# A head's bonus sum from a rounded high and low part, in two passes instead of one fp32 matmul

## The chip, the cores and the metric

The kernel runs on one core of a Trainium2 chip. The metric is the time of one execution on the device in microseconds (us), the median of the runs shown. The engines are TensorE (PE in the profile, with its weight loads listed apart as PEld), VectorE (DVE), ScalarE (ACT), GpSimd (POOL) and SyncE (SP), which issues every DMA of this kernel from one queue in order. An engine executes its own instructions in the order in which they stand.

## The reference, cut to what matters

One layer of a hybrid trunk is computed for 1024 prompt tokens and 128 sample tokens (8 requests of 16). Branch A is an RWKV-7 time mixing with 16 heads of 64 channels. Of it, this case is about one line, the bonus:

```python
y, S = wkv7_scan(wkv0.astype(f32), r_h, w_h, kh_h, a_h, v_h, kt_h)
...
yn = yn * gn_w.astype(f32) + gn_b.astype(f32)
bonus = jnp.sum(r_h * kt_h * r_bonus.astype(f32), axis=-1, keepdims=True) * v_h
o_a = (yn + bonus.reshape(B_, T, WIDTH_A)).astype(x.dtype) * jax.nn.silu(z_a)
```

For each token and head the products r * kt * r_bonus are summed over the head's 64 channels, and the sum multiplies the value vector v. Besides this there are the combined input projection (81 blocks of 128 columns), the delta-rule scan, a short-convolution branch, three output projections, a gate and norms.

## The kernel before, in words

Activations lie with channels on the 128 partitions and tokens along the free axis. Branch A is worked in 24 steps: 8 pairs of heads (j), and for each pair three token blocks, 512 prompt tokens, the 128 sample tokens and the other 512 prompt tokens (`BLOCKS`). A step goes through coroutines: `prep` (projections k, r, v, z, the decay, then `keys`), `scores`, `values`, `inverse` (a block inverse in levels), `chain` (the recurrence, chunk by chunk of 64 tokens) and `tail`. Beside them run `conv` (the convolution branch, 8 times four projections) and, when that is through, `gates_b` (six projections of the merge gates). The dense matmuls of `prep`, `conv` and `gates_b` are the filling between the dependent matmuls of the chain.

The order of PE in this first stage is written out by `go()`: a planner that holds a clock `pe[0]`. `spent` adds a price for each matmul to it (by columns; fp32 at a quarter of the speed of everything else), each coroutine yields how long its next piece must wait, and `go()` takes the first stream that is ready, or else filling. So a change of a price in `spent` moves what is taken later. The other engines, and PE after the first stage, are ordered by the framework's scheduler.

The bonus goes as follows. `keys` writes `rkt` = r * r_bonus * kt on DVE (L494), a tile of one buffer. `values` later sums it over each head's channels with one fp32 matmul against `onesb`, a 128x128 matrix of two blocks of ones (L553; in the profile all matmuls but transposes have line L92, and this one is `psb<-rkt,cpk`), and DVE multiplies v by the result (L555).

Weights come in through `load_w` (L142): a staging tile `wst` of the ring with two buffers, one DMA of 512 KB, a cast to a high fp16 part on ACT (L148) and the rest as a low part on DVE (L149). The two small decay matrices of a pair come through `load_lora` (L341): four DMAs into `lw`, a tile of its own with one buffer, and the same split (L352, L353).

The second stage (from L946 on) has the remaining merge gates (`gate`, tiles `dgb` and `dga`), the projections `dense_r` of branch B (`ob`), branch A (`oa`) and the output (`oc`). Its operands are split by `split_r` into a high part in the rounded fp32 type (F32R) and a low part that is the difference (L955, L957), and its matmuls run on these. Its tiles lie in the memory that the first stage gave back, so the loads of `ob` start when the last tail of the first stage is through.

Of the kernel before, what the change touches and what calls it, by code (L numbers as in the profile page):

```python
# [9 lines left out]
F32 = mybir.dt.float32  # L10
F16 = mybir.dt.float16
F32R = mybir.dt.float32r
I32 = mybir.dt.int32
AF = mybir.ActivationFunctionType
ALU = mybir.AluOpType
# [4 lines left out]
KT = 8  # L20
# [3 lines left out]
RN = 512  # L24
# [42 lines left out]
def build(nc, tc, I, O):  # L67
    with ExitStack() as top:
        _build(nc, tc, I, O, top)


def _build(nc, tc, I, O, top):
    V, A, G, PE, SP = nc.vector, nc.scalar, nc.gpsimd, nc.tensor, nc.sync
# [5 lines left out]
    def spent(lhsT, rhs, f32):  # L79
        rows, m, n = lhsT.shape[0], cols(lhsT), cols(rhs)  # L80
        mode = (64 if rows <= 64 else 128, 64 if m <= 64 else 128)
        t = 2 * max(n / 1.2, m / 1.2) if f32 else max(n / 2.4 + 2, 28)
        if mode != (128, 128):
            t /= 2
        if mode != pe[1] and pe[1] is not None:
            t += 100
        pe[1] = mode
        pe[0] += t / 1000

    def mm(out, lhsT, rhs, start, stop):  # L90
        spent(lhsT, rhs, lhsT.dtype == F32)
        PE.matmul(out, lhsT, rhs, start=start, stop=stop)  # L92

    def tr(out, in_, ident_):
        pe[0] += 0.14
        PE.transpose(out, in_, ident_)
# [16 lines left out]
    def P(n, i):  # L113
        o, w = PN[n]
        return par[:, o + i:o + i + 1]
# [36 lines left out]
    wcur = [None, 6]  # L152
# [36 lines left out]
    rk = ExitStack()  # L189
# [11 lines left out]
    onesb, seq4, sm_p, sm_s, i64h, scan_p, scan_s = (C[n] for n in ("onesb", "seq4", "sm_p", "sm_s", "i64", "scan", "scan_s"))  # L201
# [6 lines left out]
    def cload():  # L208
        SP.dma_start(shs, I["shift"])
        SP.dma_start(packs[0], I["c_pack"])  # L210
        SP.dma_start(packs[1], I["c_packh"])
        SP.dma_start(cvs, I["conv"])

    wk = rk.enter_context(tc.tile_pool(name="wkv", bufs=2))
    cvp = rk.enter_context(tc.tile_pool(name="cvp", bufs=1))
    wcur[0] = rk.enter_context(tc.tile_pool(name="wpool", bufs=2))
    st_ = rk.enter_context(tc.tile_pool(name="stg", bufs=1))

    def tt(pool, tag, nm, bufs, n=RBUF):
        return pool.tile([128, n], F32, tag=tag, name=nm, bufs=bufs)  # L220
# [108 lines left out]
    def pair(j):  # L329
        if j not in pairs:  # L330
            pairs[j] = s = St()
            s.w, s.lora = {}, False
        return pairs[j]
# [7 lines left out]
    def load_lora(j):  # L341
        s = pair(j)
        if s.lora:
            return
        s.lora = True
        lw = st_.tile([128, 2, 128], F32, tag="lw", name=f"lw{j}", bufs=1)
        for hv in range(2):
            for q in range(2):
                SP.dma_start(lw[hv * 64:hv * 64 + 64, q, :], I["w_lora"][j, q * 64:q * 64 + 64, :])
        s.lwh = st_.tile([128, 2, 128], F16, tag="lwh", name=f"lwh{j}", bufs=2)  # L350
        s.lwl = st_.tile([128, 2, 128], F16, tag="lwl", name=f"lwl{j}", bufs=2)
        A.activation(s.lwh, lw, AF.Copy, scale=WS)  # L352
        V.scalar_tensor_tensor(out=s.lwl, in0=lw, scalar=WS, in1=s.lwh, op0=ALU.mult, op1=ALU.subtract)  # L353
# [8 lines left out]
    def hold(us):  # L362
        bank[bank.index(min(bank))] = pe[0] + us

    def prep(f):

        j, g = f.j, f.g
        f.s = s = pair(j)
        load_lora(j)
        if g == 0:  # L370
            s.sst = wk.tile([128, 8, 64], F32, tag="sst", name=f"sst{j}", bufs=1)
# [85 lines left out]
        if ahead:  # L457
            load_lora(j + 1)
# [8 lines left out]
    def keys(f, kh, kt, b2, r, pb, pi):  # L467
        j = f.j
        blk = o, n = f.blk
        smp, nch, npr, nm = f.smp, f.nch, f.npr, f.nm  # L470
        yield lambda: S_open.at == 3 and (f.i < 1 or steps[f.i - 1].kb_done)
        ar = wk.tile([128, nch, 2, 64], F32, tag="ar", name="ar" + nm, bufs=3)
        kb = wk.tile([128, npr, 4, 64], F32, tag="kb", name="kb" + nm, bufs=1)
        ar4 = ar.rearrange("p (c e) x t -> p c (e x) t", e=2)
        if smp:
            for dst, src, t0 in ((1, kh, 0), (0, r, 1)):
                for c in range(2):
                    x = dst if c == 0 else 1 - dst
                    V.tensor_tensor(out=ar[:, c, x, :].rearrange("p (s t) -> p s t", t=16),
                                    in0=src[:, c * 64:c * 64 + 64].rearrange("p (s t) -> p s t", t=16),  # L480
                                    in1=pb[:, 4 * c:4 * c + 4, t0:t0 + 16], op=ALU.mult)
        else:
            p4 = pb.rearrange("p (c e) t -> p c e t", e=2)
            s4 = lambda x: x.rearrange("p (c e t) -> p c e t", e=2, t=64)
            V.tensor_tensor(out=ar4[:, :, 1:3, :], in0=s4(kh), in1=p4[:, :, :, 0:64], op=ALU.mult)
            V.tensor_tensor(out=ar4[:, :, 0:4:3, :], in0=s4(r), in1=p4[:, :, :, 1:65], op=ALU.mult)
        pr2 = lambda x: x.rearrange("p (c e t) -> p c e t", e=2, t=64)
        pr1 = lambda x: x.rearrange("p (c t) -> p c t", t=128)
        V.tensor_tensor(out=kb[:, :, 0:4:3, :], in0=pr2(kt), in1=pr2(pi), op=ALU.mult)
        V.scalar_tensor_tensor(out=kb[:, :, 1:3, :].rearrange("p c e t -> p c (e t)"), in0=pr1(b2), scalar=0.5,  # L490
                               in1=pr1(pi), op0=ALU.mult, op1=ALU.mult)

        f.rkt = tt(wk, "rkt", "rkt" + nm, 1, RN)[:, :n]
        V.scalar_tensor_tensor(out=f.rkt, in0=r, scalar=P("rb", j), in1=kt, op0=ALU.mult, op1=ALU.mult)  # L494
        f.ar, f.kb = ar, kb

    def scores(f):
# [28 lines left out]
    def values(f):  # L526

        smp, nch, npr, nm = f.smp, f.nch, f.npr, f.nm
        kb, v, scx = f.kb, f.v, f.scx

        kbt = f.kbt = wk.tile([128, nch, 128], F32, tag="kbt", name="kbt" + nm, bufs=2)
        for c0 in range(0, nch, 4):
            yield 0.0, 1
            pk = psp.tile([128, 512], F32, tag="p", name=f"pk{nm}_{c0}")
            cn = min(4, nch - c0)
            for c in range(c0, c0 + cn):
                tr(pk[:, (c - c0) * 128:(c - c0 + 1) * 128],
                   kb[:, c // 2, 2 * (c % 2):2 * (c % 2) + 2, :].rearrange("p a b -> p (a b)"), ident)
            hold(1.2)
            A.activation(kbt[:, c0:c0 + cn, :].rearrange("p c f -> p (c f)"), pk[:, :cn * 128], AF.Copy)  # L540

        f.kb_done = True
        vu = f.vu = wk.tile([128, nch, 128], F32, tag="vu", name="vu" + nm, bufs=2)
        vu4 = f.vu4 = vu.rearrange("p (c e) f -> p c e f", e=2)
        yield 0.0
        pv = psa.tile([128, 512], F32, tag="a", name="pv" + nm)
        for i in range(npr):
            tr(pv[:, i * 128:(i + 1) * 128], v[:, i * 128:(i + 1) * 128], ident)
        pv3 = pv[:, :npr * 128].rearrange("p (c f) -> p c f", f=128)
        A.activation(vu4[0:64, :, 0, :], pv3[0:64], AF.Copy)  # L550
        A.activation(vu4[64:128, :, 1, :], pv3[64:128], AF.Copy)
        psb = psa.tile([128, 512], F32, tag="a", name="psb" + nm)
        mm(psb[:, :npr * 128], onesb, f.rkt, start=True, stop=True)  # L553
        f.bv = v
        V.tensor_tensor(out=v, in0=v, in1=psb[:, :npr * 128], op=ALU.mult)  # L555
        yield 1.6, 1
        x0p = psp.tile([128, 8, 64], F32, tag="p", name="x0" + nm)[:, :2 * npr, :]
        for p in range(npr):
            for h, H in enumerate(HS):
                for e in range(2):  # L560
                    mm(x0p[HS[1 - e], h * npr + p, :], scx[HS[e], h, p, e, :], vu[HS[e], 2 * p + e, H],
                       start=True, stop=True)
        hold(1.5)
        x04 = x0p.rearrange("p (h c) v -> p c h v", h=2)
        for e in range(2):
            A.activation(vu4[HS[1 - e], :, e, :].rearrange("p c (h v) -> p c h v", h=2), x04[HS[1 - e]], AF.Copy)
        f.x_done = True
# [277 lines left out]
    for j in range(8):  # L845
        for g in range(3):
            f = St()
# [10 lines left out]
    load_q(0, "k")  # L858
    wl = load_w(I["w_in"][T_L], "l")
    cload()  # L860
    load_lora(0)
    cws[0] = load_w(I["w_in"][T_C], "C0")
    load_q(0, "r")
# [85 lines left out]
    op = top.enter_context(tc.tile_pool(name="op", bufs=1))  # L949
# [51 lines left out]
    for j in range(KT):  # L1001
# [3 lines left out]
        for blk in BL3:  # L1005
            o, n = blk
            ps = dense_r(w, obs, blk, f"ob{j}_{o}")
            V.scalar_tensor_tensor(out=ms[j][:, o:o + n], in0=ms[j][:, o:o + n], scalar=1.0, in1=ps,
                                   op0=ALU.add, op1=ALU.mult)
# [14 lines left out]
    for j in range(KT):  # L1024
        w = load_wr(I["w_oa"][j], f"a{j}")
        g = gts[j]
        for blk in BL3:
            o, n = blk
# [233 lines left out]
```

## Time and profile before

| | |
|---|---|
| median of 3 runs | 1888.74 us (1888.63 to 1889.81) |
| the profiled execution | 1887.54 us, of it 1885.7 us span |
| PE busy | 1795.6 us, 95% of the span |
| DVE, ACT, POOL busy | 1250.5, 815.2, 210.8 us |
| the fp32 matmuls `psb` | 24 (16 of 512 columns, 8 of 128), each listed as two passes |

The page's first part gives the busy time of each engine. Its second part cuts the span in 40 slices and gives tenths of each, with the granted clock of TensorE below. The chain of waits (part 4) is followed back from the last instruction. In a timeline a row has its start, its length, engine, line, operation, what is written from what, how many instructions are merged in the row, and in brackets the idle time before it with what ended it. Matmuls overlap: a row's length is longer than its distance to the next row, and it is the distance that counts as the engine's time.

### The profile page before, as it was taken

The numbers are of one execution on the slowest core, as the hardware profiler recorded it, in microseconds if no ns is written. First come the engines' busy times: TensorE is split into PE (matmuls) and PEld (weight loads), VectorE is DVE, ScalarE is ACT, GpSimd is POOL, SyncE is SP. The second block draws the span as 40 slices with busy tenths as digits, with TensorE's granted clock in tenths as the row PEclk, the third lists the DMA queues.
The fourth block names the chain that finished last, engine by engine and source line by source line (L and its number), as shares of the span: only waits on it lengthen the run. The fifth ranks groups of instructions, "written<-read, shape, count | busy, mean of one in ns | idle before, by whom it ended". The sixth has DMA issues, their size and how long they took to land.

```text
span 1885.7 us, 37719 instructions
## 1 busy us (share of the span) xinstructions
PE 1795.6 (95%) x15326; PEld 1242.4 (66%) x15326; DVE 1250.5 (66%) x3181; ACT 815.2 (43%) x1871; POOL 210.8 (11%) x333
## 2 busy tenths in 40 slices
PE   5999999999999999999999999999999999999997
PEld 2555665565666666566566556565499777999865
DVE  5577887788688788788788878861422411545566
ACT  6454463554555446446446446442311311333332
POOL 1001121111112111111101101100000011200000
PEclk9999999999999999999999999999999999999998
DMA  6011102011111101101100200221512410242012
GB/s 223 12 35 49 53 17 76 22 33 54 36 33 48 52 31 42 60 31 36 63 31 24 76 29 16 64 86 64 170 58 65 133 45 23 85 157 91 13 32 79
DMA packets 45198, 110.65 MB, mean 59 GB/s; under 512 B 6368, under 2 KB 21344, under 8 KB 45024
## 3 DMA queue, kind: packets, MB, share of 16 engines
q1 hardware_dynamic: 45024, 108.24, 17.9%
q8 instruction: 120, 1.97, 0.4%
q14 instruction: 54, 0.44, 0.1%
HBM read 87.94 MB, written 20.28 MB: 57 GB/s over the span
## 4 chain that ended last, share of the span: by engine, by line
PE 66%; DVE 20%; ACT 7%; DMA 3%; issue 2%; POOL 1%; SPq 0%; DVEq 0%; ACTq 0%
PE ob L92 5%; PE oc L92 5%; PE oa L92 5%; PE dr L92 4%; PE pg L92 4%; PE dz L92 4%; PE dga L92 4%; PE dgb L92 4%; PE dk L92 3%; PE dB L92 3%; PE dzb L92 3%; PE dv L92 3%; PE u L92 2%; PE dC L92 2%; PE dx L92 2%
## 5 line engine op out<-in xcount | busy, mean ns | idle before, releaser
L92 PEld LDWEIGHTS <-whip 128*128 128x128 f16 x1536 | 132.7, 99 | 72.1 <-issue 6.5
L687 POOL TENSOR_SCALAR Spt<-sbd,pt 128x128 f32<-128x128 f32 x128 | 91.3, 713 | 612.0 <-DVE sbd L706 611.0
L706 DVE SCALAR_TENSOR_TENSOR sbd<-u,pt,Spt 64x64 f32<-64x64 f32 x256 | 72.1, 282 | 68.7 <-PE u L92 65.7
L92 PEld LDWEIGHTS <-wlop 128*128 128x128 f16 x768 | 75.5, 98 | 61.8 <-issue 2.2
L92 PE MATMUL dgb<-hx,whigb 128*128 128x512 f16 (+1 forms) x480 | 110.4, 326 | 3.9 <-ACT ms L993 3.5
L627 ACT ACTIVATE bdgt<-ig 64x512 f16<-64x512 f32 (+1 forms) x208 | 106.5, 512 | 2.7
L92 PE MATMUL dB<-hx,whiB 128*128 128x512 f16 (+1 forms) x384 | 90.5, 331 | 4.4 <-ACT sho L233 4.4
L92 PE MATMUL dx<-hx,whiX 128*128 128x512 f16 (+1 forms) x384 | 90.1, 328 | 2.8 <-ACT sho L240 2.8
L92 PE MATMUL dC<-hx,whiC 128*128 128x512 f16 (+1 forms) x384 | 89.9, 328 | 2.1 <-ACT sho L233 2.1
L92 PE MATMUL dzb<-hx,whiZ 128*128 128x512 f16 (+1 forms) x384 | 88.1, 326 | 3.4 <-ACT sho L233 1.7
L92 PE MATMUL dv<-hx,whip 128*128 128x512 f16 (+1 forms) x384 | 90.1, 329 | 0.9 <-DVE zb L829 0.9
L694 ACT ACTIVATE yst<-c 64x128 f32<-64x128 f32 x144 | 38.9, 270 | 119.4 <-DVE xs L693 117.6
L92 PE MATMUL dz<-hx,whip 128*128 128x512 f16 (+1 forms) x384 | 90.5, 329 | 0.0
L92 PE MATMUL dr<-hx,whip 128*128 128x512 f16 (+1 forms) x384 | 90.0, 329 | 0.0
L92 PE MATMUL dk<-hx,whip 128*128 128x512 f16 (+1 forms) x384 | 88.1, 326 | 0.0
L92 PEld LDWEIGHTS <-pg 128*128 128x128 f16 x768 | 65.7, 99 | 27.7 <-issue 3.2
L620 ACT ACTIVATE gt<-ig 128x512 f16<-128x512 f32 (+1 forms) x104 | 54.2, 521 | 67.1 <-PE ig L92 66.6
L628 DVE CAST_PREDICATED tt<-cph,i 128x512 f16<-128x512 uint16 (+1 forms) x104 | 61.8, 594 | 29.9 <-PE i L92 26.0
L700 ACT ACTIVATE vu<-u 64x64 f32<-64x64 f32 x288 | 62.7, 218 | 39.8 <-PE u L92 36.2
L92 PE MATMUL dgb<-hx,wlogb 128*128 128x512 f16 (+1 forms) x240 | 74.4, 326 | 0.0
L634 DVE CAST_PREDICATED tn<-cph,i 128x512 f16<-128x512 uint16 (+1 forms) x104 | 61.3, 589 | 9.1 <-PE i L92 8.8
L92 PEld LDWEIGHTS u<-xs,tm 128*128 128x128 f32 x288 | 51.7, 192 | 22.6 <-DVE xs L693 5.4
(332 smaller groups left out, 4898.3 us busy)
## 6 DMA issues: line engine op xcount, KB each, us to landing
wstp<-i_w_in SPq DMA_DIRECT2D x32, 512.0 KB, 3.5
wstgb<-i_w_in SPq DMA_DIRECT2D x10, 512.0 KB, 3.5
xt<-i_x SPq DMA_DIRECT2D x9, 512.0 KB, 6.1
ob_d<-zb SPq DMA_DIRECT2D x8, 576.0 KB, 2.9
ostb<-ob_d SPq DMA_DIRECT2D x24, 192.0 KB, 2.6
osta<-oa_d SPq DMA_DIRECT2D x24, 192.0 KB, 2.5
xr<-i_xT SPq DMA_DIRECT2D x8, 576.0 KB, 3.6
wstC<-i_w_in SPq DMA_DIRECT2D x8, 512.0 KB, 3.5
```

The lines of the kernel that those rows point to most:

```text
L92: PE.matmul(out, lhsT, rhs, start=start, stop=stop)
L620: A.activation(Gt, pg, AF.Copy, scale=-1.0)
L627: A.activation(Gb[R, :, R], pg[R], AF.Copy, scale=-1.0)
L628: V.copy_predicated(out=Tt, mask=bc(lvt[:, b, :]).bitcast(U16), data=p1)
L634: V.copy_predicated(out=Tn, mask=bc(lv[:, b, :]).bitcast(U16), data=p2)
L687: G.tensor_scalar(out=Spt, in0=S, scalar1=pt[:, c:c + 1], scalar2=None, op0=ALU.mult)
L694: A.activation(yst[Vh, p, :], pc[Vh, 0:128], AF.Copy)
L700: A.activation(vu[Uh, c, H], pu[H, H], AF.Copy, scale=-1.0)
L706: V.scalar_tensor_tensor(out=S2[H, H], in0=pu[H, 128 + h * 64:192 + h * 64], scalar=pt[H, c:c + 1], in1=Spt[H, H], op0=ALU.mult, op1=ALU.add)
```

## The change

The product r * r_bonus * kt is written over r itself. ACT then copies it into a tile `rkh` in the rounded fp32 type, and POOL takes the difference into `rkl`. The sum over channels is two matmuls, of `rkh` and of `rkl`, against `onesr`, a copy of `onesb` in the rounded type that ACT makes once near the start. To make room, `lw` loses its own tile: it takes one of the two buffers of the staging ring `wst`.

```diff
@@ load_lora
-        lw = st_.tile([128, 2, 128], F32, tag="lw", name=f"lw{j}", bufs=1)
+        lw = wcur[0].tile([128, KT, 128], F32, tag="wst", name=f"lw{j}", bufs=2)[:, 0:2, :]
@@ keys
-        f.rkt = tt(wk, "rkt", "rkt" + nm, 1, RN)[:, :n]
-        V.scalar_tensor_tensor(out=f.rkt, in0=r, scalar=P("rb", j), in1=kt, op0=ALU.mult, op1=ALU.mult)
+        V.scalar_tensor_tensor(out=r, in0=r, scalar=P("rb", j), in1=kt, op0=ALU.mult, op1=ALU.mult)
+        f.rkt = [wk.tile([128, RN], F32R, tag="rk" + q, name="rk" + q + nm, bufs=1)[:, :n] for q in "hl"]
+        A.activation(f.rkt[0], r, AF.Copy)
+        G.tensor_tensor(out=f.rkt[1], in0=r, in1=f.rkt[0].bitcast(F32), op=ALU.subtract)
@@ values
-        mm(psb[:, :npr * 128], onesb, f.rkt, start=True, stop=True)
+        for q in range(2):
+            mm(psb[:, :npr * 128], onesr, f.rkt[q], start=(q == 0), stop=(q == 1))
@@ before the first stage's loads
     cload()
+    onesr = wk.tile([128, 128], F32R, tag="onesr", name="onesr", bufs=1)
+    A.activation(onesr, onesb, AF.Copy)
     load_lora(0)
```

For `spent` the matmuls are no longer fp32, so that the planner's price for a bonus sum of 512 columns is about half of what it was, and everything after it is laid anew. Three places show it.

On PE in the first step's `values` stood one matmul `psb` on `rkt` and the fp32 ones in `cpk`, between the transposes `pv` of v and the next projection `dk`:

```order
L92 MATMUL dk_1_886<-hx,wlop_8_235 128x128
L96 MATMUL pk_0_4_893<-ident,kb_0_762 128x128 x4
L96 MATMUL pv_0_900<-ident,v_0_559 128x128 x4
L92 MATMUL psb_0_907<-rkt_0_767,cpk 128x512
L92 LDWEIGHTS whip_8_234
L92 MATMUL dk_1_886<-hx,whip_8_234 128x128
```

In the same place there are now two, and their neighbours are the same:

```order
L92 MATMUL dk_1_891<-hx,wlop_8_235 128x128
L96 MATMUL pk_0_4_898<-ident,kb_0_764 128x128 x4
L96 MATMUL pv_0_905<-ident,v_0_561 128x128 x4
L92 MATMUL psb_0_912<-rkh_0_770,onesr 128x512
L92 MATMUL psb_0_912<-rkl_0_771,onesr 128x512
L92 LDWEIGHTS whip_8_234
L92 MATMUL dk_1_891<-hx,whip_8_234 128x128
```

One fp32 matmul became two of the rounded type; PE's order has 24 rows more in all.

On PE in the chain of the last step (pair 7, second prompt block), chunk 1, the matmul `c` (the state times the keys) and the first matmul `u` of the chunk had nine matmuls of the gate `dgb` between them; these are the last five of the nine, with `u` behind them:

```order
L92 MATMUL dgb_512_17360<-hx,whigb_17285 128x512
L92 LDWEIGHTS whigb_17285
L92 MATMUL dgb_512_17360<-hx,whigb_17285 128x512
L92 LDWEIGHTS wlogb_17286
L92 MATMUL dgb_512_17360<-hx,wlogb_17286 128x512
L92 LDWEIGHTS whigb_17285
L92 MATMUL dgb_512_17360<-hx,whigb_17285 128x512
L92 LDWEIGHTS whigb_17285
L92 MATMUL dgb_512_17360<-hx,whigb_17285 128x512
L92 LDWEIGHTS wlogb_17286
L92 MATMUL dgb_512_17360<-hx,wlogb_17286 128x512
L92 MATMUL u_2_1_17382<-xs_139,tm_2_17272 128x128
```

Now three stand there, and they belong to a gate of the second stage:

```order
L92 MATMUL c_2_1_17657<-sbd_124,ar_2_16897 128x128
L92 LDWEIGHTS wlogb_17833
L92 MATMUL dgb_0_17836<-hx,wlogb_17833 128x512
L92 LDWEIGHTS whigb_17832
L92 MATMUL dgb_0_17836<-hx,whigb_17832 128x512
L92 LDWEIGHTS whigb_17832
L92 MATMUL dgb_0_17836<-hx,whigb_17832 128x512
L92 MATMUL u_2_1_17663<-xs_139,tm_2_17628 128x128
```

The planner's own filling (the six gates of `gates_b`) is used up earlier: before, chunks 6 and 7 of this last chain are filled so thinly (three, two and four gate matmuls between the three matmuls of a chunk), now chunks 0 to 7 are. Behind it, from the last transposes `py` of the last tail to the first full run of `ob`, there stood 221 gate matmuls before (5 and three times 72), and 155 now (11 and two times 72); 45 matmuls of `ob` for two of its token blocks are now placed ahead of the rest, where 1 of 24 stood so before.

On SP, the DMAs of the start stood so, `lw` being the first pair's decay matrices, `wstC` and `wstp_0` the staging of the first weights of the convolution and of r, `xt` tiles of x:

```order
L212 DMA cvs<-i_conv 128x128
L349 DMA lw_248<-i_w_lora 64x128 x4
L145 DMA wstC_257<-i_w_in 128x1024
L145 DMA wstp_0_263<-i_w_in 128x1024
L261 DMA xt_269<-i_x 128x1024
L261 DMA xt_271<-i_x 128x1024
```

They stand now:

```order
L212 DMA cvs<-i_conv 128x128
L349 DMA lw_250<-i_w_lora 64x128 x4
L261 DMA xt_271<-i_x 128x1024
L145 DMA wstC_259<-i_w_in 128x1024
L145 DMA wstp_0_265<-i_w_in 128x1024
L261 DMA xt_273<-i_x 128x1024
```

One x tile moved ahead of the weights, and the four DMAs of `lw` now need a staging buffer, which the weights of k and of the decay input hold until their casts are through. On PE, seven matmuls `dC` of the first convolution weight stood ahead of the last transposes of the prologue, and one does now. For the later pairs `lw` stood on SP far ahead of the pair's other weights; now it stands behind them.

## Rows read from the trace of the kernel before

**Rows 1.** The page: busy times, the granted clock in 40 slices, and the chain of waits by engine.

```profile
PE 1795.6 (95%) x15326; PEld 1242.4 (66%) x15326; DVE 1250.5 (66%) x3181; ACT 815.2 (43%) x1871; POOL 210.8 (11%) x333
...
PEclk9999999999999999999999999999999999999998
...
PE 66%; DVE 20%; ACT 7%; DMA 3%; issue 2%; POOL 1%; SPq 0%; DVEq 0%; ACTq 0%
```

**Rows 2.** Busy time by stage: the first stage after its start, the end of its chain, and the hand-over to the second stage. Columns: stretch, its length, then busy us (and instructions) of PE, PEld, DVE, ACT and POOL, granted clock, DMA share, GB/s.

```profile
47.00:1250.00 1203.00, 1154.36 (x11220) 731.12 (x11219) 955.85 (x2519) 615.83 (x1482) 173.03 (x285) 0.99 0.14 42
1250.00:1331.00 81.00, 80.02 (x650) 46.87 (x648) 30.86 (x97) 21.55 (x58) 6.32 (x9) 1.00 0.21 74
1331.00:1376.00 45.00, 40.42 (x242) 22.12 (x242) 18.80 (x30) 19.62 (x38) 0.00 (x0) 1.00 0.52 165
```

**Rows 3.** Who PE waited for: in all, times, longest.

```profile
PE lod L92 <- DVE lrd L298: 4.4, 1, 4.4
...
PE dgb L92 <- ACT ms L993: 3.5, 2, 2.6
```

**Rows 4.** The bonus matmul: its group by form (count, busy us, mean ns), and the timeline of PE around the first one.

```profile
L92 PE MATMUL psb<-rkt,cpk 128*128 128x512 f32 x32 | 16.4, 594 | 0.0
L92 PEld LDWEIGHTS psb<-rkt,cpk 128*128 128x128 f32 x48 | 7.2, 190 | 3.5 <-DVE yc L750 3.5
...
94.06 1.02 PE L92 MATMUL psb<-rkt,cpk 128*128 128x512 f32 x2
94.92 0.27 PE L92 MATMUL dk<-hx,whip 128*128 128x128 f16 x2
```

**Rows 5.** Timeline of PE, for distances: two matmuls of the rounded type with 384 columns (`ob`), fp16 matmuls of 512 columns (`dgb`), two in the first row and one in the next, and one fp32 matmul of 128 columns (`u`, two passes) up to the next row.

```profile
1429.93 0.33 PE L92 MATMUL ob<-olb,wohb 128*128 128x384 f32 x1
1430.10 0.33 PE L92 MATMUL ob<-ohb,wolb 128*128 128x384 f32 x1
...
1304.28 0.59 PE L92 MATMUL dgb<-hx,whigb 128*128 128x512 f16 x2
1304.71 0.38 PE L92 MATMUL dgb<-hx,wlogb 128*128 128x512 f16 x1
...
1300.60 0.38 PE L92 MATMUL u<-xs,tm 128*128 128x128 f32 x2
1300.82 0.59 PE L92 MATMUL dgb<-hx,whigb 128*128 128x512 f16 x2
```

**Rows 6.** Groups by form on ACT and POOL: casts to the rounded type, copies of 512 columns, subtractions' nearest kin on POOL, and the chain's own POOL operation.

```profile
L955 ACT ACTIVATE oha<-osta 128x384 fp32r<-128x384 f32 x24 | 12.2, 520 | 21.0 <-DMA osta<-oa_d 12.8 <-PE ob L92 8.0
L540 ACT ACTIVATE kbt<-pk 128x512 f32<-128x512 f32 x32 | 18.5, 586 | 1.8 <-PE pk L96 1.6
...
L687 POOL TENSOR_SCALAR Spt<-sbd,pt 128x128 f32<-128x128 f32 x128 | 91.3, 713 | 612.0 <-DVE sbd L706 611.0
L824 POOL TENSOR_TENSOR zb<-zb,cv 128x512 f32<-128x512 f32 x16 | 21.3, 1331 | 30.1 <-DVE zb L823 17.3 <-DVE nay L138 12.4
L824 POOL TENSOR_TENSOR zb<-zb,cv 128x128 f32<-128x128 f32 x8 | 4.0, 504 | 13.1 <-DVE zb L823 13.1
```

**Rows 7.** From the product to its matmul in the step where the two lie closest: timelines of DVE and of PE.

```profile
269.31 0.35 DVE L494 SCALAR_TENSOR_TENSOR rkt<-r,par,kt 128x128 f32<-128x128 f32 x1
...
286.82 0.49 PE L92 MATMUL psb<-rkt,cpk 128*128 128x128 f32 x2 [0.48 <-DVE yc L750]
```

**Rows 8.** A POOL operation on two tensors and the DVE copies beside it: timelines of POOL and of DVE.

```profile
671.93 1.23 POOL L734 TENSOR_TENSOR vux<-vu,cpk 128x512 f32<-128x512 f32 x1 [12.57 <-PE pS L92]
...
672.18 1.12 DVE L598 COPY bdtn<-tn 64x512 f16<-64x512 f16 x1
673.32 0.29 DVE L599 COPY bdtn<-tn 64x512 f16<-64x512 f16 x1
```

**Rows 9.** The start: timelines of SP (issues), of DVE (the low parts that free the staging buffers of k and of the decay input) and of PE.

```profile
7.98 4.31 SPq L349 DMA_DIRECT2D lw<-i_w_lora  x4
13.43 0.33 SPq L145 DMA_DIRECT2D wstC<-i_w_in  x1
...
12.17 1.23 DVE L149 SCALAR_TENSOR_TENSOR wlop<-wstp,whip 128x1024 f16<-128x1024 f32 x1
15.03 1.22 DVE L149 SCALAR_TENSOR_TENSOR wlol<-wstl,whil 128x1024 f16<-128x1024 f32 x1
...
22.43 1.06 PE L92 MATMUL dC<-hx,whiC 128*128 128x512 f16 x2
23.28 0.63 PE L92 MATMUL dC<-hx,wloC 128*128 128x512 f16 x1
```

**Rows 10.** The end of the first stage and the hand-over: timeline of PE (the first matmul of chunks 6 and 7 of the last chain, the last tail's transposes, the full run of `ob`) and of SP (the first load for `ob`, and its last fifteen).

```profile
1317.42 0.46 PE L92 MATMUL c<-sbd,ar 128*128 128x128 f32 x2
1320.62 0.46 PE L92 MATMUL c<-sbd,ar 128*128 128x128 f32 x2
1330.86 0.66 PE L96 MATMUL py<-ident,yc 128*128 128x128 f32 x4 [0.61 <-DVE yc L761]
1373.21 0.52 PE L92 MATMUL ob<-olb,wohb 128*128 128x384 f32 x1
...
1334.76 0.33 SPq L964 DMA_DIRECT2D wstb<-i_w_ob  x1
1354.53 17.20 SPq L975 DMA_DIRECT2D ostb<-ob_d  x15
```

## The prediction

> **What bounds the kernel now.** I read the page first, then the stages, then PE's waits, and last the timelines at the places that the change touches. On the page PE is busy 1795.6 us of 1885.7, its clock stands at 9 tenths or more in all slices but the last, and the chain of waits is PE for 66%, DVE for 20% [rows 1]. By stages, the first one after its start (47 to 1250 us) has PE busy 1154.4 of 1203 us, so 48.6 us idle; the end of the chain has 1.0 us idle in 81, and the hand-over to the second stage 4.6 in 45 [rows 2]. So nearly every us of PE work that goes is a us of the end, as long as the order keeps PE fed; the single waits are small beside the long one at the start, 4.4 us for the decay input [rows 3]. DVE, ACT and POOL are busy at most 79%, 51% and 14% of the first stage [rows 2], and matter only where PE waits for them.
>
> **The change part by part.**
>
> *The matmuls of 512 columns.* One fp32 sum takes PE from 94.06 to 94.92, 0.86 us in its two passes [rows 4]. After it, there are two passes of the rounded type, which the trace does not show with 512 columns. From below: two fp16 matmuls of 512 columns take 0.43 us (1304.28 to 1304.71), 0.216 each. From above: rounded matmuls of 384 columns follow each other at 0.17 us, and 0.173 x 512/384 is 0.231 [rows 5]. Two passes are thus 0.43 to 0.46; I take 0.44, between. The saving is 0.42 us x 16 = 6.7 us (6.4 to 6.9).
>
> *The matmuls of 128 columns.* An fp32 one of two passes takes 0.22 us where it stands among others (1300.60 to 1300.82) [rows 5]. Two rounded passes are bounded from below by a quarter of the 0.43 above, 0.11, and from above by two weight loads in the open, 2 x 0.19 [rows 4]. That is -0.9 to +1.3 us for eight; the nearest row is the fp32 pass of 0.11 each, so I take 0.
>
> *The split on ACT and POOL.* ACT gets 24 casts. The nearest row is 0.52 us for 384 columns into the rounded type, a copy of 512 columns takes 0.59; 0.6 x 16 and 0.3 x 8 make 12 us. POOL gets 24 subtractions of two tensors: 1.33 us x 16 and 0.50 x 8, 25 us [rows 6]. The matmul needs both, some 2.2 us behind DVE's product; where the two lie closest there are 17 us between (269.7 to 286.8) [rows 7]. The cover holds, and the cost on this path is 0; without it, it would be 2.2 x 24 = 53 us. Queued behind a subtraction on POOL is the chain's `Spt` (0.71 us in the mean), which must be ready when DVE updates the state at the end of the chunk; a chunk takes 3.2 us even where it is packed most tightly (1317.42 to 1320.62) [rows 6, 10], so one subtraction ahead of it (1.33) still leaves it in time. The product itself costs DVE what it did. r's buffer is held until POOL has read it, 2 us longer in a ring of seven; I count nothing for it.
>
> *What POOL does to DVE.* While POOL ran an operation on two tensors (671.93, 1.23 us), a DVE copy took 1.12 us where its twin right after took 0.29 [rows 8]: 0.83 us lost. If each of 24 subtractions met one, DVE would lose 20 us, and with DVE at 20% of the chain [rows 1] the end would lose 4. Not each will meet one; I take 0.7, with 0 and 4 as ends. The Trainium skill ("GPSIMD Engine Reference", section "Key points") says that GpSimd shares its SBUF interfaces with VectorE, and contends with VectorE's instructions in a two-port mode or with two SBUF inputs. The row agrees for the copy; by the rule as written the 24 subtractions would slow the DVE operations on two tensors as well, which would put this term at its upper end, 4 us.
>
> *The start.* `lw` was issued at 7.98; it now needs the staging buffer that k's low part frees at 13.40, which `wstC` took at 13.43. `wstC` comes into the next one, free at 16.25, some 2.9 us later [rows 9]. ACT and DVE have other casts meanwhile, so not all of it reaches PE: before, PE did seven `dC` matmuls in the gaps ahead of the prologue's last transposes, now one. The six that come later cost 6 x 0.43 us at the spacing they had there (22.43 to 23.28 for two, the 1.2 GHz level of the clock), or 6 x 0.216 at the other: 2.6 or 1.3. I take 1.8, with 0 and 3.5 as ends. The later pairs' `lw`, which now stand behind other weights on SP, feed matmuls that come after a whole projection; I count nothing, and a stall there would be of the size of a cast, 1 us a pair.
>
> *The last chain.* Chunk 6 of it takes 3.20 us (1317.42 to 1320.62) [rows 10]. PE's work in it is nine gate matmuls, 9 x 0.216, and three fp32 matmuls of 0.22: 2.60. The 0.6 us of idle is what a thinly filled chunk costs. Two chunks stood so, eight do now: 6 x 0.6 = 3.6 us, from which I take a little for the first one: 3.4. Ends: 0 (if the scheduler's filling covers it) and 5.
>
> *The hand-over.* The loads for `ob` start at 1334.76, 3.9 us after the last transposes at 1330.86; the last fifteen are issued until 1371.7 and split until about 1375, 44 us after the transposes [rows 10]. PE had 221 gate matmuls for this (36 us) and stood 4.6 us [rows 2], 3.5 of it for ACT [rows 3]. Now 155 are left, 11 x 0.216 and two gates of 48 x 0.216 + 24 x 0.054 (a quarter of 0.216, for 128 columns), 25.8 us, and 45 `ob` matmuls x 0.173 = 7.8 us ahead: 33.6. If the loads take 44 us as before, PE stands 10.4; but SP's order now has the first weight of `ob` ahead of the last store, and two of the three rounds in which SP waited for a staging buffer fall together. I take 38 us for the loads, so 4 us idle in place of 4.6: -0.6. Ends: -4.6 and +5.8.
>
> *The new order.* The rest of the first stage is laid anew. It had 48.6 us idle; the distances in the chain and the inverse look alike in both orders, so 0, and 4 us to either side.
>
> Sum: -6.7 + 0 + 0.7 + 1.8 + 3.4 - 0.6 = -1.4 us. The profiled execution took 1887.54 us, so 1886.1; the median of the runs lies 1.2 us above it, so 1887.3.
>
> **The rivals.** *The work alone counts (faster).* PE bounds everything, the start's delay falls into the later wait for the decay input (4.4 us [rows 3]), and the chain's chunks are covered: -6.7 + 0.7 = -6.0, and the median is 1882.7. For it speaks PE's 95% [rows 1]; against it that the order at the end of the chain does get thinner. *The gates run out before `ob` is there (slower).* The loads take the 44 us they took, and PE has 25.8 to 33.6 us of work: 10.4 to 18 us idle in place of 4.6, +5.8 to +13.6, with the other terms (-0.8 without the hand-over) +5 to +13: 1894 to 1902, by its lower end, which has the `ob` matmuls ahead, 1893.7. It decides from loads of about 42 us after the last transposes; for it speaks that SP still goes through them three buffers at a time (15 in 17.2 us [rows 10]), against it the earlier weight. *The rounded type is not faster.* Then two passes take 0.86 us, 6.7 is missing: +5.3, 1894.0. Against it, 384 columns at 0.17 us [rows 5], where fp32 at 0.86 for 512 would be 0.64.
>
> **How the numbers follow.** A measurement of this kernel can tell 0.2%, 3.8 us, from no change. The forecast, -1.4 us with a range of its own of 1883 to 1892 from the ends of its terms, gets 0.43 and lies within 0.2%. The work alone gets 0.33 and is faster by over 0.2%. The gates running out gets 0.20, the type not being faster 0.04; both are slower by over 0.2%. The range for 8 in 10 is 1880 to 1895: below, the faster rival with some of the new order's 4 us; above, the lower end of the slower one.
>
> **What would show it.** In the groups by form, `psb` with 512 columns twice per step at distances of 0.22 to 0.23 us; PE busy in all lower by some 7 us. First `dC` run ending near 32 us instead of 30, and `lod` correspondingly. Eight chunks of the last chain about 3.2 us apart. From the last `py` to the first full `ob` some 38 us, with idle for `ob`'s parts that the waits list by name. DVE copies of over 1 us beside POOL's new line. Wrong would be the forecast if PE's idle in the first stage changed by more than 5 us, or if ACT or DVE stood waiting for a staging buffer at `lw`.

## The result and the profile after

The changed kernel takes 1913.75 us in the median (1913.51 to 1914.49, 4 runs), the kernel before 1888.68 beside it: 25.1 us or 1.4% slower, the ratio 1.0138 with a 95% interval of 1.0122 to 1.0154. Forecast was 1887.3 us in a range of 1880 to 1895, so the forecast was wrong, in size and in sign. Below is what the profile after shows, and then eleven experiments which say where the 25 us are.

The page of the changed kernel, busy times, clock and the chain of waits by engine:

```profile
PE 1794.8 (94%) x15326; PEld 1244.6 (65%) x15326; DVE 1256.5 (66%) x3181; ACT 828.4 (43%) x1896; POOL 240.1 (13%) x357
...
PEclk9999999999999999999999999999999999999998
...
PE 73%; DVE 15%; ACT 7%; issue 2%; DMA 2%; POOL 1%; SPq 0%; DVEq 0%; ACTq 0%; POOLq 0%
```

Against [rows 1] PE's busy time is nearly unchanged (1795.6 before), and the span is 26.0 us longer (1911.7 against 1885.7). So the loss is idle time of PE: 116.9 us in the place of 90.1. The page hides it: the digits of the clock are the same, and the share of PE only goes from 95% to 94%. The busy time itself should have fallen, by the 5 us that the bonus sums save (below); the mean granted clock over the whole execution is 0.986 instead of 0.991, so that other matmuls took longer.

By stages, for the first stage after its start and for the hand-over from the last transposes to `ob` (columns as in rows 2):

```profile
47.00:1250.00 1203.00, 1133.08 (x10967) 719.43 (x10966) 925.57 (x2428) 607.64 (x1454) 196.33 (x301) 0.99 0.13 41
...
1366.30:1400.00 33.70, 29.59 (x167) 15.54 (x168) 14.93 (x23) 15.32 (x29) 0.00 (x0) 0.95 0.53 167
```

The first stage has 69.9 us idle where 48.6 stood [rows 2]: here are 21 of the 26 us, at the place for which the prediction had put zero. Counted in each kernel from 47 us up to its own last transposes (1331.25 us before, 1366.64 now), it is 75.8 us instead of 49.6: 26.2 of the 26.8 us by which PE's idle time grew. The hand-over is about as forecast, 4.1 us idle instead of 4.6.

What PE waited for (us in all, times, longest), the rows that are new or have grown:

```profile
PE py L96 <- DVE yc L764: 8.5, 7, 4.6
PE dB L92 <- ACT sho L233: 6.3, 2, 3.5
...
PE lod L92 <- ACT lwh L352: 5.2, 3, 1.7
...
PE dzb L92 <- ACT sho L233: 5.0, 3, 1.8
PE dx L92 <- ACT sho L233: 4.6, 2, 3.4
...
PE lod L92 <- DVE lwl L353: 2.9, 3, 1.0
...
PE pS L92 <- POOL vux L737: 3.8, 1, 3.8
```

and the rows of before for the same matmuls, where there are any (`pS`, and `dx` for L233, have none of a us or more):

```profile
PE py L96 <- DVE yc L761: 5.7, 10, 2.0
...
PE dB L92 <- ACT sho L233: 4.4, 2, 2.3
...
PE dzb L92 <- ACT sho L233: 1.7, 1, 1.7
```

Two families stand here. `lod`, the first matmul on the decay weights, waits 8.1 us in three pairs for `lwh` and `lwl`, which are split from `lw`; before, that was no wait at all (the wait for `lrd` in [rows 3] is another one and is still there). And the convolution's projections (`dB`, `dzb`, `dx`), the tail (`py`) and the state (`pS`) wait longer than they did. For `dzb`, `dx` and `pS` this is a matter of the order: the fp32 kernel in the new order (the second experiment) has these waits too, with 5.3, 3.6 and 2.9 us. For `py` and `dB` the trace does not say so, since the whole change in the old order (the first experiment) has 8.0 and 5.9 us of them as well.

The bonus itself, PE's timeline at its first place:

```profile
95.86 0.48 PE L92 MATMUL psb<-rkh,onesr 128*128 128x512 f32 x1
96.18 0.40 PE L92 MATMUL psb<-rkl,onesr 128*128 128x512 f32 x1
96.42 0.29 PE L92 MATMUL dk<-hx,whip 128*128 128x128 f16 x2
```

The two passes take 0.56 us here from the first start to the next row (0.32 and 0.24), 0.55 in most places, against 0.86 [rows 4]. The split does what it says, and gains 0.31 us x 16 = 5.0 us. It is everything around it that loses.

### The profile page after: what moved, and what is told of

It is laid out like the page before. It is cut to its first block, busy times and chain, and to the rows that moved or that the text cites. A ratio compares the mean times of both kernels' runs of the same rounds, so it can differ in the third digit from the quotient of the medians.

```text
span 1911.7 us, 37798 instructions
## 1 busy us (share of the span) xinstructions
PE 1794.8 (94%) x15326; PEld 1244.6 (65%) x15326; DVE 1256.5 (66%) x3181; ACT 828.4 (43%) x1896; POOL 240.1 (13%) x357
## 4 chain that ended last, share of the span: by engine, by line
PE 73%; DVE 15%; ACT 7%; issue 2%; DMA 2%; POOL 1%; SPq 0%; DVEq 0%; ACTq 0%; POOLq 0%
PE ob L92 5%; PE oc L92 5%; PE oa L92 5%; PE dz L92 4%; PE dr L92 4%; PE dgb L92 4%; PE dC L92 4%; PE pg L92 4%; PE dk L92 4%; PE dga L92 4%; PE dv L92 3%; PE dB L92 3%; PE dx L92 3%; PE dzb L92 3%; PE u L92 3%
## 5 line engine op out<-in xcount | busy, mean ns | idle before, releaser
L696 DVE TENSOR_TENSOR xs<-c,vu 64x128 f32<-64x128 f32 x144 | 41.3, 287 | 40.8 <-PE c L92 38.0
```

The source lines that it names most:

```text
L696: V.tensor_tensor(out=xs[Uh, :], in0=pc[Uh, 0:128], in1=vu[Uh, c, :], op=ALU.add)
```

## The experiments

The profile leaves two theories: A, the new order of PE costs the time; B, the split itself costs it, by POOL's subtractions that block DVE or by `lw` in the staging ring. The first four runs cross the parts of the change. By the order of PE, the first has the rows of before but for the `psb` and six `dC` matmuls at the start, the second those of the changed kernel with the same exceptions.

**Whole change, old price.**

```diff
-        for q in range(2):
-            mm(psb[:, :npr * 128], onesr, f.rkt[q], start=(q == 0), stop=(q == 1))
+        spent(onesb, f.rkt[0], True)
+        for q in range(2):
+            PE.matmul(psb[:, :npr * 128], onesr, f.rkt[q], start=(q == 0), stop=(q == 1))
```

> The whole change, but the planner charges the two matmuls of a bonus sum as the one fp32 matmul before, so PE's order is that of before except the pairs of psb and six dC matmuls at the start. Theory A (the new order of PE costs the time): 1881 to 1887 us, that is the saving of 6.7 us less what the start costs. Theory B (the split itself costs it, by POOL's subtractions that block DVE and by lw in the staging ring): 1908 to 1920 us.

Measured: 1913.81 us, ratio 1.0140 (1.0119 to 1.0161). With PE's old order the whole loss is still there; theory A alone falls.

**The kernel before, new price.**

```diff
-        mm(psb[:, :npr * 128], onesb, f.rkt, start=True, stop=True)
+        for q in range(2):
+            spent(onesb, f.rkt, False)
+        PE.matmul(psb[:, :npr * 128], onesb, f.rkt, start=True, stop=True)
```

> The kernel before with its fp32 bonus and lw in its own tile, but the planner charges the bonus sum as two matmuls of the other types, so PE's order is that of the changed kernel except psb and the start. Theory A: slower than the changed kernel or about like it, 1908 to 1922 us. Theory B: 1885 to 1892 us, like before.

Measured: 1901.84 us, ratio 1.0075 (1.0051 to 1.0098), between the two. So the order alone does cost, 13.5 us, and B alone falls too.

**Only `lw` moves.**

```diff
-        lw = st_.tile([128, 2, 128], F32, tag="lw", name=f"lw{j}", bufs=1)
+        lw = wcur[0].tile([128, KT, 128], F32, tag="wst", name=f"lw{j}", bufs=2)[:, 0:2, :]
```

> The kernel before with only the staging tile lw moved into the ring wst. PE's order is that of before except six dC matmuls at the start. Theory A: 1888 to 1892 us, the start's 0 to 3.5 us. Theory B, if the staging ring is what costs: 1895 us or more, with PE waiting for lwh and lwl in several pairs.

Measured: 1917.34 us, ratio 1.0146 (1.0120 to 1.0172): the one line which looks like housekeeping costs 29 us by itself. Its trace shows how. The timelines of SP, ACT, DVE and PE around the first `lod` of pair 5 (pairs are counted from 0), and last the busy times of the stretch behind it, with columns as in [rows 2]:

```profile
789.44 2.43 SPq L349 DMA_DIRECT2D lw<-i_w_lora  x4
...
786.94 1.06 ACT L148 ACTIVATE whiX<-wstX 128x1024 f16<-128x1024 f32 x1 [2.03 <-PE dB L92]
...
792.56 1.06 ACT L148 ACTIVATE whip<-wstp 128x1024 f16<-128x1024 f32 x1 [0.63 <-PE dz L92]
793.64 0.69 ACT L226 ACTIVATE zs<-dz,zmu 128x512 f32<-128x512 f32 x1
794.23 0.41 ACT L352 ACTIVATE lwh<-lw 128x256 f16<-128x256 f32 x1
...
788.20 1.21 DVE L149 SCALAR_TENSOR_TENSOR wloX<-wstX,whiX 128x1024 f16<-128x1024 f32 x1
...
794.69 0.39 PE L92 MATMUL lod<-lrd,lwh 128*128 128x512 f16 x1 [1.95 <-ACT lwh L352]
796.16 0.43 PE L92 MATMUL lod<-lrd,lwl 128*128 128x512 f16 x1 [1.08 <-DVE lwl L353]
...
796.81 1.06 PE L92 MATMUL dC<-hx,whiC 128*128 128x512 f16 x2
797.67 0.63 PE L92 MATMUL dC<-hx,wloC 128*128 128x512 f16 x1
...
796.40:799.80 3.40, 3.40 (x38) 2.23 (x36) 1.18 (x3) 0.78 (x2) 2.13 (x3) 0.50 0.70 270
```

Read it from the top. `lw`'s DMA starts at 789.44, at the moment when DVE's `wloX` has read its staging buffer to the end (788.20 + 1.21). That buffer had been held by `wstX`, whose cast on ACT at 786.94 waited for PE's `dB`, that is for a place in the fp16 weights. So a staging buffer comes free only when PE has used up older weights, and `lw`, called after z, is the last of its pair to get one. On ACT its cast then stands behind `whip` and `zs`, and both need PE's projection `dz`; `lod` stands right behind `dz` in PE's order. PE waits 1.95 us for the high part and 1.08 for the low one, and about as long in each of six pairs (17.9 us in all). Before, ACT made the same cast 198 us ahead of its matmul in pairs 5, 6 and 7; these are the rows of pair 7, with the two `dC` behind the `lod` of pair 5:

```profile
873.26 0.40 ACT L352 ACTIVATE lwh<-lw 128x256 f16<-128x256 f32 x1
...
1071.70 0.38 PE L92 MATMUL lod<-lrd,lwh 128*128 128x512 f16 x1
...
777.46 0.59 PE L92 MATMUL dC<-hx,whiC 128*128 128x512 f16 x2
777.89 0.38 PE L92 MATMUL dC<-hx,wloC 128*128 128x512 f16 x1
```

The last three rows of the larger fence are the second half of the price. Behind the stall two `dC` matmuls take 0.86 us up to the next row instead of 0.43, and the granted clock is 0.50, the 1.2 GHz level, for 3.4 us, which costs 1.7 us of full speed. The Trainium skill ("TensorE: Matmul & The Clock Gate", section "What's actually happening") has the array's clock gated by how busy PE is; the trace agrees, as the clock falls right behind 3.0 us of waiting. With these that is 4.7 us a pair and 28 in six pairs, near the 29 measured. The other pairs bear it out: behind two more of the six stalls the clock stands at 0.50 for 3.4 us, behind three for 6.8, and from the first `lod` of pair 2 to that of pair 7 there are 766.1 us instead of 742.4, 4.7 us more for each of the five pairs. In the whole execution PE's idle time grew by 17.2 us and its busy time, which the clock lengthens, by 12.8.

**The subtraction on DVE.**

```diff
-        G.tensor_tensor(out=f.rkt[1], in0=r, in1=f.rkt[0].bitcast(F32), op=ALU.subtract)
+        V.tensor_tensor(out=f.rkt[1], in0=r, in1=f.rkt[0].bitcast(F32), op=ALU.subtract)
```

> The changed kernel with the 24 subtractions on DVE instead of POOL; PE's order is that of the changed kernel. If POOL's subtractions cost by blocking DVE or by standing ahead of vux and Spt on POOL: 8 us or more faster than the changed kernel, under 1906 us. If theory A alone holds: 1910 to 1918 us, about as the changed kernel (DVE gets 24 operations of some 0.6 us more).

Measured: 1916.73 us, ratio 1.0157 (1.0135 to 1.0178), no faster than the changed kernel. POOL's subtractions are not where the 25 us are.

That gave theory C: `lw`'s place in the staging ring costs most, the order has a cost of its own, and the split saves. Four runs took these apart. Two give `lw` its own tile again; the memory for it comes from the bonus' parts and ones in fp16.

```diff
-        f.rkt = [wk.tile([128, RN], F32R, tag="rk" + q, name="rk" + q + nm, bufs=1)[:, :n] for q in "hl"]
+        f.rkt = [wk.tile([128, RN], F16, tag="rk" + q, name="rk" + q + nm, bufs=1)[:, :n] for q in "hl"]
...
-        lw = wcur[0].tile([128, KT, 128], F32, tag="wst", name=f"lw{j}", bufs=2)[:, 0:2, :]
+        lw = st_.tile([128, 2, 128], F32, tag="lw", name=f"lw{j}", bufs=1)
...
-    onesr = wk.tile([128, 128], F32R, tag="onesr", name="onesr", bufs=1)
+    onesr = wk.tile([128, 128], F16, tag="onesr", name="onesr", bufs=1)
```

> PE's order of before, lw in a tile of its own again, the bonus split in two passes; to make room both parts and the ones are fp16 instead of the rounded fp32 type (a form that loses some bits of the low part). Theory C (lw in the staging ring is what costs most; the split itself saves what its matmuls save): 1880 to 1885 us, faster than before by 4 to 8 us. Theory B (the split on ACT and POOL costs): 1890 us or more.

Measured: 1885.66 us, ratio 0.9990 (0.9979 to 1.0000). That is just above what theory C expected, and the interval reaches 1: the split saves 2 to 3 us at best, where 4 to 8 were expected.

> As e5 but with the planner's new order. Theory C with the order's own cost as the fp32 kernel in the new order showed it (13.5 us): 1893 to 1899 us. If the new order only hurts together with the fp32 matmul, that is with a price that is wrong: 1880 to 1887 us.

Measured: 1903.72 us, ratio 1.0094 (1.0076 to 1.0111). Same instructions, other order: 18 us. That lies above both expectations, the first of which took the order's cost from the fp32 kernel.

The other two leave `lw` in the ring, but ask for it first:

```diff
             if ahead:
+                if q == "k":
+                    load_lora(j + 1)
                 load_q(j + 1, q)
...
-        if ahead:
-            load_lora(j + 1)
         z = m["z"]
```

> The changed kernel with the next pair's load_lora called right before the next pair's load of k instead of after z, so that lw takes its staging buffer ahead of the pair's four weights; PE's order is that of the changed kernel. Theory C: lod waits no more for lwh and lwl, and the time falls by 8 us of waits and by the clock's dips behind them, to 1893 to 1903 us. If the ring costs by what it does to the other weights: 1908 us or more.

Measured: 1911.00 us, ratio 1.0126 (1.0108 to 1.0144). The waits of `lod` are gone, but `py` now waits 11.0 us instead of 8.5, and only 2.8 us are won: this missed what theory C expected. The profiled execution took 1913.6 us, the longest of its four, and PE's idle time in it is 114.6 us where the changed kernel has 116.9.

> The same early load_lora with the order of before (the change with the old price). Theory C: the six waits of 3 us are gone, 1882 to 1888 us, less than before; if the ring costs by what it does to the other weights: 1900 us or more.

Measured: 1888.35 us, ratio 1.0007 (0.9995 to 1.0018). In the old order the moved call wins 25.5 us against the first experiment. Theory C expected less than the kernel before, and it is level with it; but the ring costs next to nothing once `lw` is asked for early (2.7 us more than with `lw` in its own tile, and some 2 of these are the faster fp16 form of that kernel's sums).

What was left is why the order costs. Counted in PE's order from the first bonus sum of a pair to that of the next, convolution and gates fill as much as 216 matmuls of 512 columns (192 of them, and 96 of 128 columns) in each pair of heads from the third pair on, before; in the changed kernel they alternate, 261 in one pair and 225 in the next. 216 is one of the convolution's eight rounds of four projections, so that before, each pair meets the same neighbours. The alternation depends on where the pairs are cut (from `lod` to `lod` the counts are 240 and 246), but the mean is 243 in every such count: the new plan also takes 27 more per pair. By the order's counts, without a run, the plan tips between a price of 0.50 and of 0.52 us for a bonus sum of 512 columns; the measured cost is 0.55, before was 0.85, the change charges 0.43.

```diff
-        for q in range(2):
-            mm(psb[:, :npr * 128], onesr, f.rkt[q], start=(q == 0), stop=(q == 1))
+        pe[0] += 0.55 * npr / 4
+        pe[1] = (128, 128)
+        for q in range(2):
+            PE.matmul(psb[:, :npr * 128], onesr, f.rkt[q], start=(q == 0), stop=(q == 1))
```

> The change with the early load_lora, and the planner charges a bonus sum of 512 columns with the 0.55 us that its two passes take in the trace of the changed kernel, instead of 0.43 (after) or 0.85 (before). By the order's counts, convolution and gates then fill 216 matmuls of 512 columns per pair again, as before; with 0.43 they alternate between 225 and 261. Theory E (the alternating plan is what the new order costs): 1884 to 1892 us. Theory F (any new order costs, since the rest of the kernel was fitted to the one before): 1895 us or more.

Measured: 1885.96 us, ratio 0.9991 (0.9979 to 1.0002).

> As e9 with 0.50 us in place of 0.55, which by the order's counts still gives the alternating plan of 225 and 261. Theory E: 1905 to 1914 us, like the changed kernel with early load_lora (1911). If it is under 1895, the alternation is not the cause.

Measured: 1912.46 us, ratio 1.0144 (1.0126 to 1.0163). The two kernels differ by one constant, 0.55 or 0.50, and by 26.5 us. Their first stages from 47 to 1250 us and the waits of PE, first with 0.55:

```profile
47.00:1250.00 1203.00, 1147.65 (x11218) 728.52 (x11217) 958.35 (x2519) 624.79 (x1504) 199.51 (x309) 0.99 0.14 43
...
PE dC L92 <- ACT sho L233: 7.8, 6, 1.8
...
PE py L96 <- DVE yc L766: 6.0, 5, 2.5
...
PE dB L92 <- ACT sho L233: 2.8, 1, 2.8
```

and with 0.50:

```profile
47.00:1250.00 1203.00, 1135.82 (x10983) 718.93 (x10983) 927.33 (x2434) 609.00 (x1459) 196.90 (x301) 0.99 0.13 41
...
PE py L96 <- DVE yc L766: 10.6, 7, 4.8
...
PE dB L92 <- ACT sho L233: 5.2, 2, 2.8
PE dzb L92 <- ACT sho L233: 5.0, 3, 1.8
PE dx L92 <- ACT sho L233: 4.6, 2, 3.4
...
PE pS L92 <- POOL vux L739: 3.8, 1, 3.8
```

The alternating plan has 67.2 us idle instead of 55.4, in many waits of a few us for results of ACT, DVE and POOL. Up to the last transposes of each kernel it is 72.9 us instead of 56.4, and in the whole execution PE is busy 4.8 us longer. So theory F falls: the order with 0.55 differs from that of before in many places and is level with it, while all kernels with the alternating one are slow, as theory E has it. What in that plan costs is not shown: its pairs both alternate and hold 27 more fillings each, and no run separates the two, nor was it taken apart why these pairs meet the waits.

**Both repairs at once**, fp16 parts, `lw` in its own tile and the price of 0.55:

> As e5 (fp16 parts, lw in its own tile) with the price of 0.55 us. Theory E: 1882 to 1888 us, about as e5 with 1885.7; theory F: 1893 us or more.

Measured: 1884.30 us, ratio 0.9983 (0.9971 to 0.9995), the one version whose interval lies below 1: 3 to 4 us faster than the kernel before, by the ratio and by the medians.

| `lw` | order of PE | bonus fp32 | bonus split |
|---|---|---|---|
| own tile | 216 per pair | 1888.7 (before) | 1885.7, 1884.3 |
| own tile | alternating | 1901.8 | 1903.7 |
| ring, asked for after z | 216 per pair | 1917.3 | 1913.8 |
| ring, asked for after z | alternating | | 1913.8 (the change) |
| ring, asked for before k | 216 per pair | | 1888.4, 1886.0 |
| ring, asked for before k | alternating | | 1911.0, 1912.5 |

The kernels of the right column with `lw` in its own tile have fp16 parts, whose sums are 2 us faster in all; the others have rounded fp32 ones. In this column the two causes don't add: the ring alone makes 28 us, the order alone 18 with `lw` in its own tile and 23 to 26 with `lw` asked for early, both together 28. In the alternating plan `lod` waits in three pairs and not in six, which is a part of it; why taking those three away wins so little stays open.

## Why the prediction was wrong, point by point

**The step that failed first is the later pairs' `lw`.** The prediction had it "stand behind other weights on SP", feeding matmuls "that come after a whole projection; I count nothing, and a stall there would be of the size of a cast, 1 us a pair". It measured 3.0 us of waiting and a dip of the clock in each of six pairs, 29 us alone. The error was to look at what stands between the load and its matmul on PE, and not at what the cast stands behind on ACT and DVE: the evacuation of the very projection that was to be its cover. The sign was written down, "if ACT or DVE stood waiting for a staging buffer at `lw`", as what would make the forecast wrong; in the changed kernel ACT stands 11.9 us for `lw`'s DMA, in four pairs, besides PE's 8.1 us in the three others. The other sign, PE's idle time in the first stage changed by more than 5 us, came true as well, with 21.

**The second is "the new order. ... so 0, and 4 us to either side".** It measured 13.5 us in the fp32 kernel and 18 to 26 in the split one. The distances in chain and inverse were compared and are alike; the number of filling matmuls per pair was not priced, and there the plan had changed. The bounds of 4 us were not drawn from a row.

**The 512-column sum** was sized with 0.44 us by the lower bound from fp16; it takes 0.55, so that 5.0 us are saved and not 6.7. The fp16 form of the last experiment does take 0.43. **The 128-column sum** was put at 0 within -0.9 to +1.3; it takes 0.26 to 0.28 us where the fp32 one takes 0.22 to 0.33 in the same order (the second experiment), 0.3 us saved in eight, so 0 was near.

**The split on ACT and POOL** held: the 16 subtractions take 1.30 us each, 1.33 was assumed, and no `psb` waits for them. **What POOL does to DVE** is small, as assumed: one place with 1.0 us is shown below, and without the subtractions on POOL the kernel was no faster.

**The start** was sized +1.8 us, with the six `dC` later; the first `lod` comes 1.2 us later and the first `psb` 1.8. **The last chain** came as forecast in its distances, its chunks 3.0 to 3.2 us apart but for the last one with 4.2; what they cost by themselves no run shows:

```profile
1345.31 0.46 PE L92 MATMUL c<-sbd,ar 128*128 128x128 f32 x2
...
1348.50 0.46 PE L92 MATMUL c<-sbd,ar 128*128 128x128 f32 x2
```

**The hand-over** was to cost -0.6 us, and its idle time went down by 0.5. That is partly luck, since the 4.1 us that are left are waits of a gate for ACT's `ms`, as before, and not for the parts of `ob`, as forecast; the rival in which the gates run out before `ob` is there did not happen. **The rival in which the work alone counts** was right on the split by itself, at best: with both repairs it is 3 to 4 us, not 6. Of the 10 us that PE's busy time fell in that kernel (1785.4 against 1795.6), 6.5 came back as idle time (96.6 against 90.1). The rival of a type that is not faster is out.

## What to carry to other kernels

A tile that is moved into another ring takes over that ring's queue: ask what has to be finished before its buffer comes free, and what its cast then stands behind on the casting engines, since a weight that was there 198 us early may come just too late. Where a planner's price sets an order, count what the plan puts into one period before and after; a price that moved by 0.05 us moved the time by 26. Here the measured price lay on the good side, but so did the old one, which was 0.30 us too high (1888.4 us with it and 1886.0 with the measured one): what counted was the plan that came out.

## What the runs showed of the hardware

A rounded fp32 sum of 512 columns is 0.12 us slower than an fp16 one: its first pass takes 0.32 us up to the second, the second 0.24, where the fp16 passes stand 0.22 apart. The rows of the last experiment, for comparison with those of the changed kernel above:

```profile
93.48 0.38 PE L558 MATMUL psb<-rkh,onesr 128*128 128x512 f16 x1
93.70 0.38 PE L558 MATMUL psb<-rkl,onesr 128*128 128x512 f16 x1
93.92 0.28 PE L92 MATMUL dk<-hx,whip 128*128 128x128 f16 x2
```

An operation of POOL on two tensors held up even a DVE operation on one column, at the one place where such a pair met. In the changed kernel (first two rows) and in the fp32 kernel in the new order, without the subtraction (third row):

```profile
950.86 1.65 POOL L496 TENSOR_TENSOR rkl<-r,rkh 128x512 fp32r<-128x512 f32 x1 [3.34 <-ACT rkh L495]
...
951.31 1.22 DVE L229 SCALAR_TENSOR_TENSOR v<-sho,par,v 128x1 f32<-128x1 f32 x1
```

```profile
940.95 0.21 DVE L229 SCALAR_TENSOR_TENSOR v<-sho,par,v 128x1 f32<-128x1 f32 x1
```

It took 1.22 us instead of 0.21, until POOL was through, and the projection `dx` behind it waited 3.44 us instead of 2.43. The rule of the Trainium skill that the prediction named ("GPSIMD Engine Reference", section "Key points") agrees with this. But moving all 24 subtractions to DVE brought nothing.
